# FFN gate/up products from float16 halves with scales found on the chip, all split tiles kept in DRAM

## The chip, the cores and the metric

The kernel runs on one core of one Trainium2 chip. The metric is the device time of one execution in microseconds (us), as the median of several runs.

## The reference

One inference step of an encoder layer with width 1024, for 2048 new frames and 64 frames of a running stream (2112 tokens together):

```python
h = rmsnorm(x, norm1_w)
proj = h @ w_in                       # q, k, v, z, a, b of four delta-rule heads, and pool inputs
...                                   # convolution, gated delta rule in chunks, causal pooling
x = x + concatenate([o_delta, o_pool]) @ w_out
h = rmsnorm(x, norm2_w)
x = x + (silu(h @ w_gate) * (h @ w_up)) @ w_down      # 1024 -> 2816 -> 1024
y = rmsnorm(x, normf_w)
```

All inputs and outputs are float32, and the result has to be close to that of float32 arithmetic.

## The kernel before

**Split products.** TensorE is fed with operands of reduced float32 (`F32R`). To keep float32 accuracy, each operand is split into a high half, which is the value rounded to that type, and a low half, which is the rest. Each product is made of three matmuls: high by high, high by low, low by high (the loop over `(0, 0), (0, 1), (1, 0)` in `add`, line 1650). A split takes two instructions: ACT copies the value into the high half, and DVE subtracts (`wsplit`, line 567).

**Two phases.** The first phase (four token blocks of 512, the first with the 64 extra tokens) does the input projection, the heads, the pooling and the output projection, and leaves x in DRAM. The second phase is the FFN. It goes over the tokens in three blocks of 704, each as two halves of 352 columns (`N2`). Each block goes over the 2816 hidden columns as 22 tiles of 128 (`NF`), in groups of 4, 4, 4, 4, 2, 4. `gate_up(b, f)` (line 1643) makes tile f of gate and up for block b; `down` or `down_strassen` adds a finished group into the result.

**Strassen in gate and up.** For one tile, the two token halves, the two weight matrices and the two halves of the 1024 inputs make a 2x2 block product, which is done with 7 block products instead of 8 (Strassen's scheme in Winograd's form). The seven left factors are the weight tiles `FW = ("11", "S1", "S2", "12", "S3", "S4", "22")`, where 11 and 12 come from `wg`, 22 from `wu` and the S tiles are sums; the right factors are the token tiles `FH`. Each product is 4 steps over the inputs by 3 matmuls: 12 matmuls of 128x128 by 352 columns, and 84 for a tile. The products are added up in three PSUM banks (px, py, pz); ACT and DVE combine them (g1, g2, u2), ACT makes the sigmoid from exponentials and a logarithm, and DVE multiplies (`finish`, line 1664).

**Where the weight tiles come from.** `prep_strassen` (line 621) makes the seven split tiles for hidden tile f. In the first block it loads four raw tiles of 128x512 (256 KB each), POOL makes the four sums, and ACT and DVE split all seven. The four split S tiles (512 KB each) are then stored into DRAM (`gsd`). In the second and third block the S tiles are loaded back, and the other three are loaded raw and split again. Raw tiles sit in `wraw` (4 buffers) and `wraw2` (3 buffers), split tiles in `wsp` and `wsp2` (4 buffers each, one tile of 4 KB a partition for each product). `weights` keeps up to three plan entries ahead (`AHEAD = 3`, `weights_ahead`, line 735).

**The token tiles** are made by `stats2` (line 1430): x scaled by the norm weight `n2w` and the root mean square, combined by POOL, and written to DRAM (`hpd`). `load_h` (line 1519) loads and splits them: ACT the high half, DVE or POOL the low one.

**The order of the work.** No engine runs in the order of the program text. Every instruction is noted (`Machine.note`, line 107) with a rank, its position in the text, and an estimate of its length (`cost`, line 147). At the end `issue` (line 190) plays the program through in its own model: each engine takes the ready instruction with the lowest rank (some, such as evictions of PSUM, are pulled ahead by `hurry`), and the order found is emitted for each engine. On the chip each engine then follows its list in that order and waits where something is late. For TensorE `pick` (line 288) treats reduced float32 matmuls (kind "r") as the bulk, which goes in order of rank, and holds other kinds back for a while to keep them together. All DMAs are issued by the SP queue, also in one list. Buffers of a pool made with `behind=True` (`f2`, used in the FFN) come free only when the last instruction on the first phase's own buffers is done.

Of the kernel before, what the change touches and what calls it, by code (L numbers as in the profile page):

```python
# [18 lines left out]
P = 128  # L19
D = 1024  # L20
# [44 lines left out]
class Machine:  # L65
# [81 lines left out]
    def cost(self, op, name, out, ins):  # L147
# [4 lines left out]
        if op.eng == "tensor":  # L152
            dt = ins[0].dtype
            if name == "transpose":
                op.kind, op.ldw, op.occ = "f", 0.11, 0.109
            elif dt == F32:
                op.kind, op.ldw, op.occ = "f", 0.11, 0.012 + 1.651e-3 * n
            elif dt == F32R:
                op.kind, op.ldw, op.occ = "r", 0.11, 0.008 + 0.4335e-3 * n
            else:  # L160
                op.kind, op.ldw, op.occ = "h", 0.055, 0.003 + n / 2.4e3
            op.lat = op.occ + 0.2
            return
# [13 lines left out]
        elif op.eng == "scalar":  # L177
            op.lat = (0.16 if ps else 0.2) + 0.84e-3 * n + 0.095 * max(0, len(ins) - 1)
            op.occ = op.lat - 0.1
            if "accum_out" in op.call[2]:  # L180
                op.lat, op.occ = 0.6, 0.3
# [106 lines left out]
    def pick(self, ready, t, wait):  # L288

        others = sorted(x for x in ready if x[2].kind != "r")  # L290
        if others:
            first = others[0]
            held = self.last == "r" and len(others) < len(ready) and t < min(x[2].ready + self.hold(x) for x in others)
            if self.last == "r" and not held and len(others) < len(ready):
                until = min(x[2].ready + (SOON if x[0] < 0 else HOLD[1]) for x in others)
                held = any(t < x[0] <= until and x[2].kind != "r" for x in wait)
            if held:
                first = min(x for x in ready if x[2].kind == "r")
# [9 lines left out]
    def run(self, op, t):  # L308
        op.start = t
        if op.eng == "tensor":  # L310

            free, kind = self.free["tensor"], op.kind
            if self.last == kind and op.ready <= free:
                op.start = max(t, self.at + op.ldw)
            elif kind == "r":
                if op.ready <= free:
                    op.start = max(op.ready, free - (0.028 if self.last == "h" else 0.081))
                op.occ, op.lat = op.occ + 0.087, op.lat + 0.087
            elif self.last == "h":
# [50 lines left out]
def hybrid_kernel(ctx, tc, a, o):  # L370
# [88 lines left out]
    gsd = {nm: dpool.tile([NF, P, 1024], F32, tag=f"g{nm}", name=f"g{nm}") for nm in KEEP}  # L459
# [35 lines left out]
    n1w, n2w, nfw = (nw[:, i * KT : (i + 1) * KT] for i in range(3))  # L495

# [63 lines left out]
    def wtiles(nm, second=False):  # L560
# [3 lines left out]
        return (lambda: pool.tile([P, 512], F32, tag="wraw" + x, name=f"wr{nm}_{at}", bufs=3 if second else 4),  # L564
                lambda: pool.tile([P, 2, 512], F32R, tag="wsp" + x, name=f"ws{nm}_{at}", bufs=4))
# [5 lines left out]
    def prep():  # L571
# [43 lines left out]
        while due and due[0][0] != key:  # L615
            k, done = due.pop(0)
            for dst, t in done:
                nc.sync.dma_start(out=dst, in_=flat(t))
            stored.add(k)

    def prep_strassen(key):

        q = {f"{i}{j}": a[nm][key[1]][:, (j - 1) * 512 : j * 512]
             for i, nm in ((1, "wg"), (2, "wu")) for j in (1, 2)}
        raw, t, old = {}, {}, key in stored or key[1] in PRE_GU

        def get(nm, src):
            raw[nm] = wtiles(nm)[0]()
            nc.sync.dma_start(out=raw[nm], in_=q[src])

        if old:
            for i, nm in enumerate(FW):
                t[nm] = wtiles(nm, i % 2 == 1)[1]()
                if nm in gsd and key[1] in PRE_GU:
                    for j in range(2):
                        nc.sync.dma_start(out=t[nm][:, :, 256 * j : 256 * j + 256].bitcast(F32),
                                          in_=gpd[key[1], j][PRE_NM.index(nm)].rearrange("p (q n) -> p q n", q=2))
# [14 lines left out]
        gt(out=raw["S4"], in0=raw["12"], in1=raw["S2"], op=ALU.subtract)  # L652
        for i, nm in enumerate(FW):
# [267 lines left out]
    nc.sync.dma_start(out=consts, in_=a["consts"])  # L921
    names = {}
# [36 lines left out]
    idbf = cp1.tile([P, P], BF16, tag="idbf", name="idbf")  # L959
    nc.vector.tensor_copy(idbf, ident)  # L960
# [18 lines left out]
    class Front:  # L979
# [43 lines left out]
        def all(self):  # L1023
# [32 lines left out]
            mm(gb[:, : 2 * C], idbf, bc(negm2 if self.h is None else negm, 2, C), start=False, stop=True,  # L1056
# [462 lines left out]
    def load_h(b, names):  # L1519
        for nm in names:  # L1520
            for k in range(4):
# [3 lines left out]
                else:  # L1525
# [4 lines left out]
                    out=t[:, 1], in0=raw, in1=t[:, 0].bitcast(F32), op=ALU.subtract)  # L1530
# [14 lines left out]
    hA = [bp.tile([P, 6, 2, N2], F32R, tag=f"h{i}", name=f"hA{i}") for i in range(2)]  # L1545
# [17 lines left out]
    for nm in FH[3:]:  # L1563
        t = f2.tile([P, 4, 2, N2], F32R, tag=f"h{nm}", name=f"hB{nm}")
# [78 lines left out]
    def gate_up(b, f):  # L1643
# [14 lines left out]

        def sigmoid(e, x):
            act(e, x, AF.Exp, scale=-1.0)  # L1660
# [146 lines left out]

HOLD = 0.3, 3.0, 0.6
# [26 lines left out]
PRE_NM = ("S3", "S1", "S2", "S4")  # L1835
SLACK = 0.6
KEEP = ("S1", "S2", "S3", "S4")
# [118 lines left out]
```

## Time and profile before

| | us |
|---|---|
| median of 3 runs | 2296.19 (2296.04 to 2296.88) |
| span of the profiled execution | 2295.8 |
| first phase, up to the first gate/up matmul | 933.0 |
| FFN, block 0 (to the first gate/up matmul of block 1) | 449.7 |
| FFN, block 1 | 448.8 |
| FFN, block 2, to its last gate/up matmul | 422.4 |
| the rest: last down product, final norm | 41.9 |

The profiled execution's own time is its span and what lies around it; the span is 0.4 us under the median of the runs. The profile names instructions by engine (PE is the matmul array, PEld its weight loads, DVE VectorE, ACT ScalarE, POOL GpSimd, SP the queue of DMAs) and by what they write and read: `px<-hA,ws` is a matmul into px from the token tile hA and the weight tile ws (`wsS` are the S tiles, `wsd` those of the down product, `hr`, `g` and `u` the gating, `hq` its split factors, `y` the result). Nearly all instructions have the line 285, where the program emits them, so the names tell them apart. Numbers in names are left out. Reduced float32 is shown as f32 on PE. The busy time of overlapping instructions counts once.

### The profile page before, as it was taken

The page shows a single profiled execution, that of the slowest core. Times are in us where ns is not written, and L with a number is a line of the kernel's source. Part 1 is how long each engine was busy: PE and PEld are TensorE (multiplying, and loading weights), DVE is VectorE, ACT ScalarE, POOL GpSimd, SP SyncE. Part 2 cuts the span into 40 slices and gives each one's busy share as a digit, 9 for nine tenths or more (in the row PEclk, how much of TensorE's full clock was granted, in tenths as well). Part 3 has the DMA queues.
Part 4 walks back from the last instruction along what each step waited for, and adds up shares of the span by engine and source line. Part 5 has one row for each costly group of instructions (what it writes and reads, how often), then busy time and mean ns, then how long its engine had stood idle before and what let it go on. Part 6 is the DMA issues. An engine that isn't in the chain of part 4 may idle for free.

```text
span 2295.8 us, 41549 instructions
## 1 busy us (share of the span) xinstructions
PE 2271.8 (99%) x14518; PEld 2132.1 (93%) x14518; DVE 1711.3 (75%) x3129; ACT 1342.1 (58%) x3039; POOL 833.4 (36%) x893
## 2 busy tenths in 40 slices
PE   8999999999999999999999999999999999999998
PEld 8898898888787888999999999999999999999998
DVE  8989876685678896788888786866667768666576
ACT  6986866684769864565446366554334574353344
POOL 3425342453247450565434236622111453010112
PEclk9999999999999999999999999999999999999999
DMA  8755586578476767866776578778765776666653
GB/s 295 263 182 193 199 294 234 191 238 277 159 245 232 212 212 254 304 247 247 272 260 238 185 264 292 248 266 302 234 198 199 263 271 230 209 216 224 210 195 103
DMA packets 256514, 536.96 MB, mean 234 GB/s; under 512 B 30000, under 2 KB 94000, under 8 KB 256304
## 3 DMA queue, kind: packets, MB, share of 16 engines
q1 hardware_dynamic: 255728, 533.58, 69.3%
q8 instruction: 114, 1.87, 0.3%
q14 instruction: 96, 0.79, 0.1%
q10 hardware_dynamic: 576, 0.72, 0.1%
HBM read 403.62 MB, written 130.58 MB: 233 GB/s over the span
## 4 chain that ended last, share of the span: by engine, by line
PE 88%; DVE 5%; DMA 3%; ACT 2%; issue 1%; POOL 1%; SPq 0%; DVEq 0%; POOLq 0%; ACTq 0%
PE px L285 21%; PE pp L285 17%; PE pz L285 13%; PE py L285 10%; PE dx L285 8%; PE dy L285 4%; PE d L285 3%; PE dz L285 2%; PE pk_p L285 2%; PE pt_p L285 2%; PE gr_p L285 1%; DVE y L285 1%; PE py_p L285 1%; DVE h L285 1%; DMA hpd<-xt 1%
## 5 line engine op out<-in xcount | busy, mean ns | idle before, releaser
L285 PE MATMUL pp<-h,wsp 128*128 128x512 f32 (+1 forms) x2480 | 547.9, 364 | 10.0 <-DVE wsp L285 10.0
L285 PEld LDWEIGHTS pp<-h,wsp 128*128 128x128 f32 x2480 | 401.4, 189 | 58.2 <-ACT wsp L285 9.2
L285 ACT CAST ws<-wr 128x512 fp32r<-128x512 f32 x198 | 122.1, 618 | 166.7 <-PE dx L285 55.2
L285 DVE TENSOR_TENSOR ws<-wr,ws 128x512 fp32r<-128x512 f32 x198 | 173.4, 879 | 30.9 <-ACT ws L285 27.1
L285 POOL TENSOR_TENSOR q<-hr,hr 128x352 f32<-128x352 f32 x52 | 58.0, 1116 | 369.6 <-DVE hr L285 366.8
L285 ACT CAST wsd<-wrd 128x512 fp32r<-128x512 f32 (+1 forms) x120 | 62.6, 526 | 174.8 <-PE dx L285 66.8
L285 DVE TENSOR_TENSOR y<-y,dx 128x352 f32<-128x352 f32 x240 | 121.8, 517 | 57.0 <-PE dx L285 56.0
L285 PE MATMUL pz<-op,wsp 128*128 128x288 f32 (+1 forms) x768 | 163.0, 353 | 0.0
L285 PE MATMUL px<-hA,ws 128*128 128x352 f32 x792 | 145.2, 322 | 0.0
L285 ACT ACTIVATE hr<-g 128x352 f32<-128x352 f32 x132 | 65.6, 497 | 133.7 <-DVE g L285 133.5
L285 PE MATMUL py<-hA,wsS 128*128 128x352 f32 x792 | 141.5, 322 | 2.0 <-DMA wsS<-gS 1.6
L285 PE MATMUL py<-hB,wsS 128*128 128x352 f32 x792 | 141.7, 322 | 0.0
L285 PE MATMUL pz<-hB,ws 128*128 128x352 f32 x792 | 141.0, 322 | 0.0
L285 ACT CAST TV_p<-pt_p 128x512 f16<-128x512 f32 x192 | 110.4, 589 | 49.6 <-PE pt_p L285 49.2
L285 PE MATMUL px<-hA,wsS 128*128 128x352 f32 x792 | 138.5, 322 | 0.0
L285 PE MATMUL px<-hBT,wsS 128*128 128x352 f32 x792 | 137.9, 322 | 0.2 <-ACT g L285 0.2
L285 PE MATMUL px<-hBT,ws 128*128 128x352 f32 x792 | 137.7, 322 | 0.0
L285 PEld LDWEIGHTS pz<-op,wsp 128*128 128x128 f32 x768 | 120.9, 188 | 12.1
L285 PEld LDWEIGHTS py<-hA,wsS 128*128 128x128 f32 x792 | 129.4, 188 | 2.6 <-DMA wsS<-gS 1.9
L285 PEld LDWEIGHTS px<-hA,ws 128*128 128x128 f32 x792 | 130.0, 188 | 0.1
L285 PE MATMUL dy<-hq,wsdS 128*128 128x352 f32 x672 | 129.6, 322 | 0.0
L285 PEld LDWEIGHTS py<-hB,wsS 128*128 128x128 f32 x792 | 129.4, 188 | 0.0
(697 smaller groups left out, 5777.2 us busy)
## 6 DMA issues: line engine op xcount, KB each, us to landing
wsS<-gS SPq DMA_DIRECT2D x176, 512.0 KB, 4.5
wsp<-wnd SPq DMA_DIRECT2D x126, 512.0 KB, 3.8
gS<-wsS SPq DMA_DIRECT2D x88, 512.0 KB, 4.9
wsdS<-dsd SPq DMA_DIRECT2D x88, 512.0 KB, 4.4
wr<-in_wg_dram SPq DMA_DIRECT2D x132, 256.0 KB, 3.5
wnd<-wsp SPq DMA_DIRECT2D x42, 512.0 KB, 5.0
wrd<-in_wd_dram SPq DMA_DIRECT2D x68, 256.0 KB, 2.7
xd<-x2d SPq DMA_DIRECT2D x96, 176.0 KB, 4.1
```

The lines of the kernel that those rows point to most:

```text
L285: getattr(getattr(self.nc, op.eng), name)(*args, **kw)
```

## The change

- Weight and token tiles of gate and up become float16 halves. The seven weight tiles are kept in pairs, four buffers of 4 KB a partition for a hidden tile instead of seven (`new` in `prep_strassen`).
- To keep the halves in the range of float16, weights are multiplied by a power of two s for each hidden tile, and the norm weight `n2w` by another. They are found on the chip by `scale_of`: ACT squares the four raw tiles with accumulated sums, DVE copies the sums into bfloat16, PE adds them over the partitions (one matmul with a matrix of ones for each column of sums, one column wide), ACT takes logarithm and exponential to get the inverse root, and DVE masks the result down to its exponent. The split becomes an ACT copy with scale s and a DVE `scalar_tensor_tensor` (raw x s - high). The scale is taken out again in the gating: the exponential gets `neg` as its scale, and the two products of `finish` become `scalar_tensor_tensor` with `inv`.
- The first block stores all seven split tiles (three times 512 KB and once 256 KB for a hidden tile); the later blocks only load them.
- Raw tiles of odd hidden tiles get four buffers of their own (`graw`), and `wraw2` gets six buffers instead of three.
- In the planner, 16-bit matmuls of at least 288 columns are a second bulk kind "b", and the estimate for ACT instructions with accumulation depends on their size. A bfloat16 identity of the first phase falls away; its matmul uses the float16 one.

```diff
-                op.kind, op.ldw, op.occ = "h", 0.055, 0.003 + n / 2.4e3
+                op.kind, op.ldw, op.occ = "b" if n >= WIDE else "h", 0.055, 0.003 + n / 2.4e3
...
-        others = sorted(x for x in ready if x[2].kind != "r")
+        others = sorted(x for x in ready if x[2].kind not in BULK)
...
-    gsd = {nm: dpool.tile([NF, P, 1024], F32, tag=f"g{nm}", name=f"g{nm}") for nm in KEEP}
+    gsd = {i: dpool.tile([NF, P, 2048 if i < 6 else 1024], F16, tag=f"g{i}", name=f"g{i}") for i in range(0, 7, 2)}
...
+    def scale_of(out, squares, n, top, ps):
+
+        cols = cpool.tile([P, 4], BF16, tag="sqb", name=f"sqb{machine.n}", bufs=2)[:, :n]
+        nc.vector.tensor_copy(cols, squares)
+        for i in range(n):
+            mm(ps[:, :1], ones_b, cols[:, i : i + 1], start=i == 0, stop=i == n - 1)
+        act(out, ps[:, :1], AF.Ln, bias=tiny, scale=1.0 / top**2)
+        act(out, out, AF.Exp, scale=-0.5)
+        bits = out.bitcast(mybir.dt.int32)
+        nc.vector.tensor_single_scalar(bits, bits, 0x7F800000, ALU.bitwise_and)
+
+    def weigh_norm():
+
+        sq = cpool.tile([P, 4], F32, tag="sq", name="sqn", bufs=2)
+        junk = cpool.tile([P, KT], F32, tag="junkn", name="junkn")
+        act(junk, n2w, AF.Square, accum_out=sq[:, :1])
+        scale_of(nscale, sq[:, :1], 1, 2.0**13 / D**0.5, bank(0, "nscale"))
+        ts(n2w, n2w, nscale, None, ALU.mult)
...
-        return (lambda: pool.tile([P, 512], F32, tag="wraw" + x, name=f"wr{nm}_{at}", bufs=3 if second else 4),
-                lambda: pool.tile([P, 2, 512], F32R, tag="wsp" + x, name=f"ws{nm}_{at}", bufs=4))
+        return (lambda: pool.tile([P, 512], F32, tag="wraw" + x, name=f"wr{nm}_{at}", bufs=6 if second else 4),
+                lambda: pool.tile([P, 2, 2, 512] if pair else [P, 2, 512], dt, tag="wsp" + x, name=f"ws{nm}_{at}", bufs=4))
...
-        if old:
-            for i, nm in enumerate(FW):
-                t[nm] = wtiles(nm, i % 2 == 1)[1]()
...
-                elif nm in gsd:
-                    nc.sync.dma_start(out=flat(t[nm]), in_=gsd[nm][key[1]])
-                else:
-                    get(nm, nm)
-                    wsplit(t[nm], raw[nm], 512, nc.vector)
-            return t
-        for nm, src in (("11", "11"), ("S1", "21"), ("22", "22"), ("12", "12")):
-            get(nm, src)
+        def new(i):
+            pair = wtiles("".join(FW[i : i + 2]), i % 4 == 2, F16, True)[1]()
+            t.update((nm, pair[:, j]) for j, nm in enumerate(FW[i : i + 2]))
+            return pair.rearrange("p i q n -> p (i q n)")[:, : 1024 * len(FW[i : i + 2])]
+
+        if key in stored:
+            for i in range(0, 7, 2):
+                nc.sync.dma_start(out=new(i), in_=gsd[i][f])
+            return t
+        sq = cpool.tile([P, 4], F32, tag="sq", name=f"sq{f}", bufs=2)
+        junk = wq["pool"].tile([P, 512], BF16, tag="junk", name=f"junk{f}")
+        for i, (nm, src) in enumerate((("11", "11"), ("S1", "21"), ("22", "22"), ("12", "12"))):
+            raw[nm] = wq["pool"].tile([P, 512], F32, tag="graw", name=f"gr{nm}_{f}", bufs=4) if f % 2 else wtiles(nm)[0]()
+            nc.sync.dma_start(out=raw[nm], in_=q[src])
+            act(junk, raw[nm], AF.Square, accum_out=sq[:, i : i + 1])
...
+        scale_of(s, sq, 4, 2.0**13, psp.tile([P, 512], F32, tag="mm", name=f"ws{f}", bufs=PSM))
+        ts(neg, s, nscale, -1.0, ALU.mult, ALU.mult)
+        nc.vector.reciprocal(neg, neg)
+        ts(inv, neg, -1.0, None, ALU.mult)
...
         for i, nm in enumerate(FW):
-            t[nm] = wtiles(nm, i % 2 == 1)[1]()
-            wsplit(t[nm], raw[nm], 512, nc.vector)
-        due.append((key, [(gsd[nm][key[1]], t[nm]) for nm in FW if nm in gsd]))
+            if i % 2 == 0:
+                kept.append((gsd[i][f], new(i)))
+            hi, lo = t[nm][:, 0], t[nm][:, 1]
+            act(hi, raw[nm], AF.Copy, scale=s)
+            stt(lo, raw[nm], s, hi, ALU.mult, ALU.subtract)
+        due.append((key, kept))
...
-    hA = [bp.tile([P, 6, 2, N2], F32R, tag=f"h{i}", name=f"hA{i}") for i in range(2)]
+    hA = [bp.tile([P, 6, 2, N2], F16, tag=f"h{i}", name=f"hA{i}") for i in range(2)]
...
         def sigmoid(e, x):
-            act(e, x, AF.Exp, scale=-1.0)
+            act(e, x, AF.Exp, scale=neg)
...
         def finish(i, g, u):
             e = raw[:, i]
-            tt(e, e, g, ALU.mult)
-            tt(e, e, u, ALU.mult)
+            stt(e, e, inv, g, ALU.mult, ALU.mult)
+            stt(e, e, inv, u, ALU.mult, ALU.mult)
...
+BULK, WIDE = ("r", "b"), 288
```

More of the change, by code (lines that the diff above doesn't have):

```diff
@@ L312, in run @@
             free, kind = self.free["tensor"], op.kind
-            if self.last == kind and op.ready <= free:
+            narrow = ("b", "h")
+            if (self.last == kind or kind in narrow and self.last in narrow) and op.ready <= free:
                 op.start = max(t, self.at + op.ldw)
@@ L316, in run @@
                 if op.ready <= free:
-                    op.start = max(op.ready, free - (0.028 if self.last == "h" else 0.081))
+                    op.start = max(op.ready, free - (0.028 if self.last in narrow else 0.081))
                 op.occ, op.lat = op.occ + 0.087, op.lat + 0.087
-            elif self.last == "h":
+            elif self.last in narrow:
                 op.occ, op.lat = op.occ + 0.054, op.lat + 0.054
```

48 lines of the change are left out of this document (26 added, 22 removed).

## The prediction, made before the changed kernel was run

> **What bounds the kernel now.** I read the busy shares first, then four stretches of the span, then the waits of PE, and last the single starts of matmuls.
>
> ```profile
> span 2295.8 us, 41549 instructions
> PE 2271.8 (99%) x14518; PEld 2132.1 (93%) x14518; DVE 1711.3 (75%) x3129; ACT 1342.1 (58%) x3039; POOL 833.4 (36%) x893
> ```
>
> ```profile
> 933.00:1016.50 83.50, 83.10 (x516) 82.31 (x515) 72.92 (x94) 57.08 (x120) 45.59 (x35) 1.00 0.83 297
> 1016.50:1382.70 366.20, 365.79 (x2281) 365.22 (x2280) 304.04 (x493) 185.46 (x383) 160.19 (x123) 1.00 0.69 243
> 1382.70:1831.50 448.80, 446.87 (x2782) 445.39 (x2781) 314.24 (x561) 221.69 (x469) 140.15 (x137) 1.00 0.75 247
> 1831.50:2253.90 422.40, 422.05 (x2632) 421.52 (x2631) 281.36 (x504) 200.89 (x419) 92.41 (x88) 1.00 0.68 221
> ```
>
> ```profile
> PE py L285 <- DMA wsS<-gS: 1.6, 1, 1.6
> PE dz L285 <- DVE y L285: 0.9, 3, 0.3
> ```
>
> The stretches (columns: bounds and length, then busy us of PE, PEld, DVE, ACT, POOL, then clock, DMA share, GB/s) are the FFN up to the last gate/up matmul: block 0 in two parts, block 1, block 2. In all four PE lacks 3.1 us of 1320.9, at full clock, and the list of its waits from 935 to 2260 us holds these two and 0.6 us more. So here the time is the number of matmuls times the step from one start to the next. The weight loads are busy all the time as well, but they lie under the matmuls: the steps below grow with the columns, not with the loads.
>
> **The step that is removed and the one that comes.** Gate and up are 7 products of 12 matmuls for each of 22 tiles in 3 blocks: 5544 matmuls of 352 columns, in groups of 792 like the first row. The timeline rows after it are start, length, instruction and count.
>
> ```profile
> L285 PE MATMUL px<-hA,ws 128*128 128x352 f32 x792 | 145.2, 322 | 0.0
> ```
>
> ```profile
> 889.74 43.45 PE L285 MATMUL pz<-op,wsl 128*128 128x512 f32 x191
> 933.03 2.08 PE L285 MATMUL px<-hA,ws 128*128 128x352 f32 x12
> 934.95 2.08 PE L285 MATMUL py<-hA,wsS 128*128 128x352 f32 x12
> ```
>
> ```profile
> 415.04 0.63 PE L285 MATMUL pp<-h,wsp 128*128 128x512 f32 x2
> 415.51 0.28 PE L285 MATMUL pt_p<-Yt_p,TV_p 128*128 128x128 f16 x2
> ...
> 415.75 0.28 PE L285 MATMUL pt_p<-Yt_p,TV_p 128*128 128x128 f16 x2
> ...
> 416.14 0.22 PE L285 MATMUL pf_p<-TV_p,Wl_p 128*128 128x128 f16 x1
> 416.16 0.71 PE L285 MATMUL pp<-h,wsp 128*128 128x512 f32 x2
> ```
>
> ```profile
> 757.54 0.27 PE L285 MATMUL gb_p<-negm,idbf 128*128 128x256 bf16 x1
> 757.65 0.39 PE L285 MATMUL py_p<-TV_p,Wh_p 128*128 128x128 f16 x4
> ```
>
> Reduced float32 (shown as f32): twelve matmuls of 352 columns start within 934.95 - 933.03 = 1.92 us, 160.0 ns each; 512 columns take (933.03 - 889.74) / 191 = 226.7. The difference, 66.7 ns for 160 columns, is 0.417 ns a column, so 13.3 ns of the 160.0 are a fixed part. 16-bit operands: from the fifth to the twelfth matmul of the run at 415 us are 7 steps in 0.39 us, 55.7 ns for 128 columns. 128 x 0.417 is 53.3, so the fixed part is 2.4 ns; the 256 columns of 757.54 took 110 ns, fixed part 3.3. A 16-bit matmul of 352 columns is not in this trace. Its bounds: its columns alone, 146.7 ns, and the 128-column step scaled in proportion, 153.2. Between them I take 146.7 plus 2.4 to 3.3, 149.5, because both 16-bit rows fit it. That removes 10.5 ns x 5544 = **58.2 us** (37.7 to 73.7 by the bounds), a third of it in block 0.
>
> **What is added on PE.** First, changes of type. The down products and the norm sums stay reduced float32, and PE takes what is ready, so the two kinds alternate. The pair of 512-column matmuls ahead of the 16-bit run is 0.63 us long, the pair after it 0.71, and that pair starts 0.03 after the last 16-bit start rather than 0.056; on the way in, the last 512 columns take 0.24 to the next start and the first four 16-bit steps 0.24 rather than 0.22: some 0.08 us there and back. Going through the whole timeline after 933 us I count 143 places where a gate/up matmul and another one are neighbours, from the first to the last of these rows:
>
> ```profile
> 984.92 0.32 PE L285 MATMUL rpn<-hin,ones 128*128 128x352 f32 x1
> ...
> 2253.77 19.96 PE L285 MATMUL d<-h3l,wsd 128*128 128x352 f32 x122
> ```
>
> About 71 round trips x 0.08 = **5.7 us** (4 to 8, since the order will differ). Second, the scale: per tile of block 0 four matmuls of one column with a full 128x128 weight load. The nearest rows are the 16-bit steps (0.056 each) and the 12-column float32 matmuls below, 7 steps in 0.95 - 0.25, 0.10 each. The weights are 16 bit, so I take 0.06 x 4 = 0.25 per tile, 22 tiles **5.5 us** (4.9 to 8.8). The start gets one such chain for the norm weights, some 0.5 us (0 to 2), where PE waits anyway.
>
> ```profile
> 43.27 0.95 PE L285 MATMUL pc<-consts,Rt 128*128 128x12 f32 x8
> ```
>
> **What is added on DVE, ACT and POOL, and what covers it.** In blocks 1 and 2 every tile loses three ACT casts and three DVE splits and gets four slightly longer DVE operations; its loads fall from 4 x 512 + 3 x 256 KB to 3 x 512 + 256 KB. All that only falls, under a full PE; the one DMA wait of 1.6 us may go. In block 0 each tile gets four ACT squares with accumulator reads, a logarithm and an exponential, five DVE operations on one to four columns, seven splits as scalar_tensor_tensor, and four such in the gating.
>
> ```profile
> L285 DVE TENSOR_TENSOR y<-y,dx 128x352 f32<-128x352 f32 x240 | 121.8, 517 | 57.0 <-PE dx L285 56.0
> L285 DVE SCALAR_TENSOR_TENSOR y<-y,nw,rf 128x352 f32<-128x352 f32 x16 | 8.4, 577 | 1.5 <-ACT rf L285 1.5
> ```
>
> ```profile
> L285 DVE TENSOR_SCALAR kn_p<-kn_p x32: 155/169/783, 61.7 to 813.1; 128x2 f32<-128x2 f32 x32
> ```
>
> ```profile
> 809.50 0.20 ACT L285 ACTIVATION_READ_ACCUMULATOR ktl_p<-ptk_p 128x1 f32 x1
> 809.59 0.28 ACT L285 ACTIVATE ktl_p<-ptk_p 128x128 f32<-128x128 f32 x1
> ...
> 810.34 0.31 ACT L285 ACTIVATE kn_p<-kn_p,epsc 128x2 f32<-128x2 f32 x1
> 810.53 0.62 ACT L285 ACTIVATE osq_p__2643<-po_p__2533 128x512 f32<-128x512 f32 x1
> ```
>
> The three-operand form takes 577 ns against 517, +0.06 each, so DVE gets 11 x 0.06 + 5 x 0.17 = 1.5 us per tile. A square of 512 columns is 0.62 us long and its read 0.09 behind it (809.50 to 809.59), the two small functions 0.31 at most: ACT gets 4 x 0.6 + 0.6 = 3 us per tile. In the first six tiles that is 57 + 18 = 75 us of work for 78 us (below), in the rest of block 0 some 235 for 350. Cover is there, but thin at first.
>
> DVE is closer, because it does not work alongside POOL. Here POOL runs two sums from 948.57 to 951.72, and a DVE product that takes 0.52 undisturbed, started at 950.50, ends 0.4 after POOL's second:
>
> ```profile
> 948.57 3.15 POOL L285 TENSOR_TENSOR wrS<-wrS,wr 128x512 f32<-128x512 f32 x2
> ```
>
> ```profile
> 950.50 1.60 DVE L285 TENSOR_TENSOR hr<-hr,u 128x352 f32<-128x352 f32 x1
> ```
>
> The groups of 933 to 1016.5 us, the first six tiles with no down product between them, say how much of this there is:
>
> ```profile
> L285 DVE TENSOR_TENSOR wsS<-wrS,wsS 128x512 fp32r<-128x512 f32 x21 | 22.3, 1085 | 1.0 <-ACT wsS L285 1.0
> L285 DVE TENSOR_TENSOR ws<-wr,ws 128x512 fp32r<-128x512 f32 x16 | 18.1, 1129 | 1.9 <-ACT ws L285 1.9
> L285 DVE TENSOR_TENSOR hr<-hr,g 128x352 f32<-128x352 f32 x11 | 9.1, 824 | 0.0
> ```
>
> ```profile
> L285 POOL TENSOR_TENSOR wrS<-wrS,wr 128x512 f32<-128x512 f32 x10 | 14.8, 1484 | 1.1 <-DVE ws L285 0.7
> L285 POOL TENSOR_TENSOR r<-r,sq7n 128x352 f32<-128x352 f32 x2 | 2.5, 1253 | 0.1
> ```
>
> ```profile
> L285 DVE TENSOR_TENSOR ws<-wr,ws x198: 676/693/1791, 925.7 to 2240.9; 128x512 fp32r<-128x512 f32 x198
> L285 POOL TENSOR_TENSOR wrS<-wr,wrS x44: 1284/1571/1755, 923.1 to 1341.7; 128x512 f32<-128x512 f32 x44
> ```
>
> With the undisturbed lengths of the last two rows (0.52 and 0.89 for 352 columns): 37 splits x 0.69, 24 products and splits of the gating (the 11 shown, and 13 in two smaller groups) x 0.52, 20 sums of POOL (two groups of 10) x 1.29 and 14 norm sums (seven groups of 2) x 0.89 make 25.5 + 12.5 + 25.8 + 12.5 = 76 of 83.5 us for a resource that one of the two holds at a time. The Trainium skill, SBUF — State Buffer, section "SBUF: two separate sides", states just this: a DVE operation with two SBUF inputs and a GpSimd one take an exclusive lock for the whole instruction. The trace agrees (0.52 became 1.60), and by that rule the stall below is 7 us; by the busy share of DVE alone it would be nothing.
>
> After the change PE wants these six tiles in 83.5 - 6 x 84 x 0.0105 = 78 us, and the pair needs 76 + 53 x 0.06 = 79. Some of it can go elsewhere: the norm sums come later in the order, tiles with odd number have raw buffers of their own, and six instead of three buffers take the sums, so two tiles' sums (10 us) can run in this gap of POOL:
>
> ```profile
> 923.12 1.74 POOL L285 TENSOR_TENSOR wrS<-wr,wrS 128x512 f32<-128x512 f32 x1 [37.31 <-DMA wrS<-in_wu_dram]
> ```
>
> Against that stands the first tile: its split now waits for all four raw tiles and the scale. I put **7 us** of new PE idle into block 0 (0, if the buffers cover all, to 19.4 = 1848 x 0.0105, if the block keeps its old pace). The waits added are: PE's four small matmuls for the DVE copy of the sums of squares, with the running gate/up matmuls queued behind them; ACT's first split for the scale, with the evictions of px and py behind it; DVE for the exponential, with the additions that free PSUM behind it.
>
> **Sum.** -58.2 + 5.7 + 5.5 + 0.5 + 7.0 = -39.5 us on the span of 2295.8: 2256.3. The profiled execution took about as long as the median of 2296.19 (0.4 lies around the span), so I predict **2256 us**.
>
> **Rivals.** *Block 0 is bound by DVE, POOL and ACT.* For it: 76 of 83.5 us held already, and ACT at 75 of 78. Against it: from 1016.5 to 1382.7 DVE is busy 304 of 366, and the buffers deepen. Then block 0 keeps its pace: 2256 + 12 = 2268, to about 2285 where some of the 22 x 1.5 us of added DVE work shows too. *The chain of the scale is exposed* (slower). Square and read 0.8, copy 0.17, matmuls 0.25, logarithm and exponential 0.31 each, mask 0.17, and five hand-offs, 0 to 0.3 each by the waits of PE for DVE above, say 0.15: 2.8 us per tile of block 0. If PE stands in front of its small matmuls, or the first split comes too late, in all 22 tiles, that is 61 us in place of the 7: 2310. It outweighs the gain from 46.5 / 22 = 2.1 us per tile. Against it: tiles are prepared some three steps ahead, and with paired buffers eight slots hold two tiles rather than one. *The type gives nothing.* If the fixed 13.3 ns belong to the 352-column accumulation and not to the type, only the added work stays: 2296 + 5.5 + 0.5 + 7 = 2309. The two 16-bit rows speak against it. The Trainium skill, FP8 and Floating Point Precision, section "TensorE Precision Notes", speaks for it: half-precision and reduced float32 both pass the array in the same narrow internal form. By that alone the sum is 2309; the rows, 55.7 and 110 ns, do not bear it out as a rule on time. *More is gained*: the step near 147 and no idle, 2235 to 2243.
>
> **Chances.** Forecast (2243 to 2267) 0.66; block 0 bound by the other engines 0.18; exposed chain 0.05; no gain from the type 0.04; more gained 0.07. The range that leaves 2 in 10 out at most: 2243, where the 16-bit step is 149 and nothing stalls, to 2277, where block 0 gains nothing and the small matmuls and type changes are at their upper bounds (8.8 and 8). Changes within 0.2% (4.6 us) can't be told from none: faster 0.89, same 0.03, slower 0.08.
>
> **What would show it.** The seven gate/up groups must appear as f16 with starts 149 to 150 ns apart, 1.79 us per twelve; 153 or more would break the main term. Blocks 1 and 2 (448.8 and 422.4 us) should each shorten by about 19.4 - 2 us, with PE full. Block 0 (449.7) should shorten by less, 3 to 12 us, with PE waits on the scale's copy, the splits or POOL's sums of 7 us together; if PE waits there for 20 us, the other engines bind. If the first gate/up matmul starts several us after the last output projection, the scale of the first tile is exposed.

## The result, and the profile after

The changed kernel takes 2259.51 us in the median of 4 runs (2257.41 to 2261.72), the kernel before beside it 2296.53 (2296.04 to 2300.72). The ratio, estimated from all runs and so not quite the quotient of the two medians, is 0.9834, with a 95% interval of 0.982 to 0.9847: 1.7% faster, 3.5 us above the predicted 2256. The profiled run has a span of 2259.3, 36.5 us less than the 2295.8 before.

The first fence holds the head of the page after, the second the stretches of the FFN (block 0, block 1, block 2 to its last gate/up matmul; columns as in the prediction).

```profile
span 2259.3 us, 41012 instructions
```

```profile
936.55:1385.38 448.83, 437.74 (x2874) 334.39 (x2875) 386.89 (x689) 315.12 (x703) 191.27 (x157) 0.99 0.70 238
1385.38:1817.02 431.64, 428.97 (x2788) 330.68 (x2787) 276.83 (x496) 193.45 (x409) 138.53 (x144) 1.00 0.64 207
1817.02:2217.42 400.40, 400.40 (x2623) 303.09 (x2622) 240.93 (x436) 168.56 (x350) 78.07 (x79) 1.00 0.56 175
```

Against 449.7, 448.8 and 422.4 before, the blocks changed by -0.9, -17.2 and -22.0; the rest takes 41.9 as before. The first gate/up matmul starts 3.5 us later (936.55 against 933.03). So blocks 1 and 2 gave all of the gain, and block 0, with a third of the matmuls, almost none: PE lacks 448.83 - 437.74 = 11.1 us there, where it lacked 0.8 before.

PE's timeline of the changed kernel in block 1 (start, length, instruction, count):

```profile
1455.27 1.95 PE L285 MATMUL px<-hA,wsS 128*128 128x352 f16 x12
1457.06 1.95 PE L285 MATMUL pz<-hB,wsS 128*128 128x352 f16 x12
...
1462.43 1.95 PE L285 MATMUL px<-hBT,ws 128*128 128x352 f16 x12
1464.10 1.24 PE L285 MATMUL dx<-hq,wsd 128*128 128x352 f32 x6
1465.18 1.13 PE L285 MATMUL dy<-hq,wsdS 128*128 128x352 f32 x6
1466.15 1.12 PE L285 MATMUL dz<-hq,wsd 128*128 128x352 f32 x6
```

Twelve float16 matmuls take 1457.06 - 1455.27 = 1.79 us, 149.2 ns each. In the same stretch six reduced float32 ones of the same size take 1466.15 - 1465.18 = 0.97, about 161 ns each: the difference is the type's. The change of type costs next to nothing here: from 1462.43 to 1465.18 are 2.75 us, and twelve steps of 149.2 and six of 161 are 2.76.

The way into block 0, from the timelines of PE, ACT, DVE and POOL of the changed kernel (a last bracket is the idle time before and what ended it):

```profile
919.75 15.12 PE L285 MATMUL pz<-op,wsl 128*128 128x512 f32 x66
934.72 0.51 PE L285 MATMUL ws<-sqb,onesb 128*128 128x1 bf16 x8
936.55 0.47 PE L285 MATMUL px<-hA,ws11S 128*128 128x352 f16 x2 [1.33 <-ACT ws11S L285]
...
938.43 0.45 PE L285 MATMUL pz<-hB,wsS 128*128 128x352 f16 x1 [0.80 <-ACT wsS L285]
938.68 2.99 PE L285 MATMUL px<-hA,ws11S 128*128 128x352 f16 x10
```

```profile
935.00 0.26 ACT L285 ACTIVATE wscale<-ws,tiny 128x1 f32<-128x1 f32 x1 [1.81 <-PE ws L285]
```

```profile
930.21 0.39 DVE L285 CAST sqb<-sq 128x4 bf16<-128x4 f32 x1 [2.39 <-ACT junk L285]
933.23 1.10 DVE L285 CAST sqb<-sq 128x4 bf16<-128x4 f32 x1 [2.63 <-ACT junk L285]
```

```profile
933.02 1.29 POOL L285 TENSOR_TENSOR grS<-grS,gr 128x512 f32<-128x512 f32 x1
```

Tile 0's sums of squares are in bfloat16 at 930.60. Its four small matmuls stand in PE's list beside those of tile 1, whose cast is done at 934.33, behind the output projection, and start at 934.72; ACT finds the scale from 935.00 and splits, and PE starts 1.83 us late. The other 1.7 us of the 3.5 lie before: the last output projection starts at 891.2 for 889.5 before, and in the profiles below, whose first phase does the same work, anywhere from 889.7 to 893.6.

The waits of PE in block 0 (total, times, longest), and the longest of them as PE and ACT see it:

```profile
PE dx L285 <- ACT wsd L285: 2.7, 1, 2.7
PE px L285 <- ACT g L285: 2.5, 3, 1.9
PE px L285 <- ACT ws11S L285: 2.2, 3, 1.3
PE rpn L285 <- ACT hin L285: 1.3, 1, 1.3
```

```profile
1157.08 1.65 PE L285 MATMUL px<-hA,ws11S 128*128 128x352 f16 x10
...
1161.86 0.24 PE L285 MATMUL ws<-sqb,onesb 128*128 128x1 bf16 x4
1164.79 0.59 PE L285 MATMUL dx<-hq,wsd 128*128 128x352 f32 x2 [2.69 <-ACT wsd L285]
...
1166.31 0.43 PE L285 MATMUL dz<-hq,wsd 128*128 128x352 f32 x1 [0.42 <-DVE g L285]
1166.58 3.64 PE L285 MATMUL px<-hA,wsS 128*128 128x352 f16 x12
```

```profile
1161.11 0.85 ACT L285 CAST hq<-hr 128x352 fp32r<-128x352 f32 x2
...
1162.91 0.26 ACT L285 ACTIVATE wscale<-ws,tiny 128x1 f32<-128x1 f32 x1
...
1164.12 0.61 ACT L285 CAST wsd<-wrd 128x512 fp32r<-128x512 f32 x1
...
1165.27 0.43 ACT L285 COPY g<-px 128x352 f32<-128x352 f32 x1
```

PE has finished px by 1158.73, but ACT works through sigmoids, casts for the down product (hq, wsd), the scale and a split first and copies px out at 1165.27; the wait of 2.69 us ends with the cast of wsd. Of what the change added, only the scale (1162.91 to 1163.40) stands between. PE has little else to do from 1162.1 to 1166.6, and then twelve matmuls take 3.45 us (the next starts at 1170.03) instead of 1.79, at a granted clock that has fallen to half:

```profile
1166.60:1169.60 3.00, 3.00 (x12) 1.60 (x12) 3.00 (x6) 2.52 (x5) 0.45 (x1) 0.51 0.44 146
```

### The profile page after: what moved, and what is told of

The parts are those of the page before. It is cut to its first block, busy times and chain, and to the rows that moved or that the text cites. A ratio compares the mean times of both kernels' runs of the same rounds, so it can differ in the third digit from the quotient of the medians.

```text
span 2259.3 us, 41012 instructions
## 1 busy us (share of the span) xinstructions
PE 2222.5 (98%) x14607; PEld 1786.3 (79%) x14607; DVE 1639.1 (73%) x3111; ACT 1358.8 (60%) x3131; POOL 803.9 (36%) x893
## 3 DMA queue, kind: packets, MB, share of 16 engines
q8 instruction: 114, 1.87, 0.3%
## 4 chain that ended last, share of the span: by engine, by line
PE 86%; DVE 6%; ACT 3%; DMA 2%; issue 1%; POOL 1%; SPq 0%; DVEq 0%; POOLq 0%; ACTq 0%
PE px L285 18%; PE pp L285 17%; PE pz L285 13%; PE dx L285 9%; PE py L285 9%; PE dy L285 5%; PE d L285 3%; PE dz L285 2%; PE pk_p L285 2%; PE pt_p L285 2%; PE gr_p L285 1%; PE py_p L285 1%; DVE y L285 1%; DVE wsS3S L285 0%; DVE hq L285 0%
## 5 line engine op out<-in xcount | busy, mean ns | idle before, releaser
L285 PEld LDWEIGHTS <-wsS 128*128 128x128 f16 x1584 | 154.2, 98 | 86.4 <-issue 4.5
L285 PEld LDWEIGHTS <-ws11S 128*128 128x128 f16 x1584 | 151.0, 98 | 88.3 <-ACT ws11S L285 3.8
L285 PEld LDWEIGHTS <-wsS3S 128*128 128x128 f16 x1584 | 154.2, 98 | 81.3
L285 PE MATMUL px<-hA,ws11S 128*128 128x352 f16 x792 | 138.5, 315 | 3.1 <-ACT ws11S L285 2.2
L285 PE MATMUL dx<-hq,wsd 128*128 128x352 f32 x560 | 137.1, 332 | 2.7 <-ACT wsd L285 2.7
L285 PE MATMUL px<-hA,wsS 128*128 128x352 f16 x792 | 131.6, 315 | 2.5 <-ACT g L285 2.5
L285 PE MATMUL py<-hA,ws11S 128*128 128x352 f16 x792 | 133.7, 313 | 0.3 <-DVE hr L285 0.2
L285 PE MATMUL dx<-hq,wsdS 128*128 128x352 f32 x672 | 132.1, 326 | 1.0 <-DVE hq L285 1.0
L285 PE MATMUL pz<-hB,wsS 128*128 128x352 f16 x792 | 131.5, 313 | 0.9 <-ACT wsS L285 0.8
L285 PE MATMUL py<-hB,wsS3S 128*128 128x352 f16 x792 | 132.2, 313 | 0.0
```

Of the source, the lines that this page charges most:

```text
L285: getattr(getattr(self.nc, op.eng), name)(*args, **kw)
```

## The experiments

Theory: the type gives the gain in every block, and in block 0 finding the scales eats it, as a wait (the chain of small steps is late) or as work (the engines have more to do). Rivals: block 0 is held by DVE and POOL whether or not scales are found; the planner's or the buffers' edits do the work. Each ratio is to the kernel before on the same chip; block 0 is counted from its first gate/up matmul to that of block 1.

**A constant scale.**

```diff
+            nc.vector.memset(s, 2.0**9)      # once, all 22 tiles; neg and inv from it
-            act(junk, raw[nm], AF.Square, accum_out=sq[:, i : i + 1])
-        scale_of(s, sq, 4, 2.0**13, ...)
```

> This kernel leaves out the finding of the weight scales: no squares, no sums of squares, no one-column matmuls, no logarithm, exponential or mask for the 22 hidden tiles; all tiles use the constant 512. The splits, the gating and the stores stay. If the finding is what keeps block 0 from getting shorter (the PE idle of 11.1 us and the start 3.5 us late), the first gate/up matmul starts at about 933, block 0 takes 434 to 437 us in place of 448.8, blocks 1 and 2 stay at 431.6 and 400.4, and the time is about 2244. If the pair DVE and POOL binds block 0 whether or not scales are found (the rival 'block 0 bound by DVE, POOL and ACT'), only the start and the small matmuls come back: about 2254.

Measured: 2245.42 us, ratio 0.9774 (0.9761 to 0.9788). Block 0 takes 435.65, PE lacks 5.7 us of it, and the first gate/up matmul follows the output projection at once. Finding the scales costs about 0.006 of 2296.5, 14 us: 13.2 in block 0 by the profiles. So the rival that DVE and POOL hold block 0 anyway is out for the 13 us; in the 5.7 that stay, the waits of PE name DVE for 4.1 and ACT for 1.5.

**The scales found, but not used.**

```diff
-        s = ...                              # of this tile
+        s = wscale[0][:, 0, f : f + 1]       # 512; the found one is left in a tile of its own
```

> Here the whole finding is still done for every tile, but nothing waits for it: splits and gating use the constant 512, as in the kernel without the finding. It separates the work of the finding from the wait for it. If the wait for the scale (its latency) is the cost, the time is that of the kernel without the finding plus the 88 one-column matmuls, some 2246. If the load on ACT and DVE is the cost, it stays near the 2259.5 of the changed kernel. My estimate is in between, 2250: the 3.5 us at the start and the first waits are latency, the waits for ACT from 940 to 1021 are load.

Measured: 2257.58, ratio 0.9822 (0.9808 to 0.9835). PE starts at once after the output projection, but block 0 takes 446.56. So most of the cost is not the wait of splits and gating for the scale but the instructions. (These still wait for one another in the engines' lists, the small matmuls for the casts and the logarithm for the matmuls; that part is not taken out here.) The difference of 1.2 thousandths to the changed kernel lies within the intervals; only the 1.83 us at the start can be seen as the wait's.

**Squares alone.**

```diff
             act(junk, raw[nm], AF.Square, accum_out=sq[:, i : i + 1])
-        scale_of(s, sq, 4, 2.0**13, ...)
```

> The constant scale again, and the sums over the partitions, the one-column matmuls, the logarithm, the exponential, the mask and the three short products are left out; only the four squares per hidden tile are done, and nothing reads their sums. It cuts the 13 us that the finding costs in block 0 into the squares (3 us of ACT per tile) and the short chain behind them. If the squares are the cost, block 0 takes 445 to 449 us and the ratio is 0.982. If the short instructions are, block 0 takes 435 to 438 and the ratio is 0.977 to 0.979; that is what the squares over a quarter of the columns, which brought nothing, let me expect.

Measured: 2247.78, ratio 0.9785 (0.977 to 0.98), block 0 438.07.

**Squares over a quarter of the columns.**

```diff
-            act(junk, raw[nm], AF.Square, accum_out=sq[:, i : i + 1])
+            act(junk[:, :128], raw[nm][:, :128], AF.Square, accum_out=sq[:, i : i + 1])
```

> The squares run over the first 128 of each raw tile's 512 columns (the target is halved, so the scale has the same size). ACT loses some 0.4 us per square, 1.6 us per hidden tile, 34 us in block 0; DVE, POOL and PE get the same instructions. If ACT's load is what costs block 0 its gain, about half of the 13 us that the finding costs there come back: block 0 at 442 to 444, the time at a ratio to the kernel before of about 0.980. If the short DVE instructions between the splits cost it (or the wait itself), block 0 stays at 446 to 449 and the ratio at 0.982 to 0.984.

Measured: 2263.22, ratio 0.985 (0.9833 to 0.9866), block 0 452.43: no gain, and above both ranges that I had given. The stretch of block 0 in these four kernels, in their order:

```profile
934.41:1370.06 435.65, 429.99 (x2795) 331.41 (x2794) 380.98 (x583) 255.09 (x499) 207.60 (x163) 1.00 0.72 249
```

```profile
936.84:1383.40 446.56, 436.10 (x2883) 335.53 (x2883) 384.82 (x693) 314.33 (x710) 203.26 (x164) 0.99 0.71 243
```

```profile
934.21:1372.28 438.07, 431.30 (x2796) 331.81 (x2795) 379.55 (x583) 305.33 (x665) 207.21 (x162) 1.00 0.72 248
```

```profile
937.14:1389.57 452.43, 438.57 (x2875) 334.25 (x2875) 378.33 (x689) 289.98 (x704) 198.26 (x157) 0.99 0.69 236
```

The squares add 305.33 - 255.09 = 50 us to ACT and 2.4 us to the block (the ratios of the two kernels, 0.9774 and 0.9785, lie within each other's intervals). The short chain behind them (casts, small matmuls, logarithm, exponential, mask, three products) adds only 314.33 - 305.33 = 9 us to ACT and 5 to DVE, and 8.5 to the block. Of these the small matmuls themselves are 2.2 (below), 3.7 are more idle time of PE (446.56 - 436.10 = 10.5 against 438.07 - 431.30 = 6.8), and in the block PE runs twice instead of once at half clock for some 3.4 us. The longest wait of the second kernel, its PE row, and ACT's rows up to it:

```profile
990.46 3.25 PE L285 MATMUL px<-hA,wsS 128*128 128x352 f16 x12 [3.79 <-ACT g L285]
```

```profile
989.17 0.50 ACT L285 ACTIVATE sq6n<-xd 128x352 f32<-128x352 f32 x1 [0.55 <-DVE hr L285]
989.96 0.45 ACT L285 COPY g<-px 128x352 f32<-128x352 f32 x1 [0.29 <-POOL r L285]
```

The copy that frees PE stands in ACT's list behind a square of the norm statistics; ACT is idle before both, by the profile until DVE and POOL are done. Such a wait does not need the short chain: the kernel with the squares alone has one of 2.93 us, for ACT's copy g too and with half clock behind it, at 978.53. That the planner's estimates, by which the squares would have been done, put the copy there is my reading and was not tested. What is shown is that the short chain costs the block more than the squares, though it is a fifth of their work on ACT; with a quarter of the squares nothing was gained. Which of the short steps costs most, and whether by the order or by the work, isn't settled.

**Three ways to place the finding better:** raw buffers of their own for the even tiles instead of the odd ones; a truer estimate of a square; both, with the chain ahead of other work.

```diff
-... if f % 2 else wtiles(nm)[0]()
+... if f % 2 == 0 else wtiles(nm)[0]()                     # even
-                op.lat, op.occ = max(0.6, op.lat + 0.1), max(0.3, op.occ)
+                op.lat, op.occ = max(0.6, op.lat + 0.1), max(0.3, op.occ + 0.23)   # square's cost
+        machine.boost = BOOST                              # ahead
         scale_of(s, sq, 4, 2.0**13, ...)
```

> The four raw buffers of their own go to the even hidden tiles instead of the odd ones, so that tile 0, the first that PE needs, loads at about 890 us, when tile 1 loads in the changed kernel, and its scale can be found under the output projection. All else is computed as before. If the late start (936.5 against 933.0) and the waits of the first tiles are the exposed scale of tile 0, the first gate/up matmul comes at 933 to 933.5 and the waits from 936 to 941 fall away: 2252 to 2255. If the load of ACT in the first six tiles sets the pace, the same idle time comes some tiles later and the time stays at 2258 to 2260.

> Only the planner's estimate of an ACT square with accumulation is changed, by 0.23 us to the 0.76 that the trace shows from one square to the next; no instruction is added or removed, only the order can differ. If the 6.2 us of PE idle from 1021.8 to 1385.4 come from an order that counts on ACT being free 0.9 us earlier per tile, the time falls by 3 to 6 us, to 2254 to 2257. If they come from the load itself, it stays within 2 us of 2259.5.

> The finding of all 22 scales stays, in a better place: raw buffers of their own for the even tiles (tile 0 first), the short chain ahead of other work, and squares planned at their measured pace. If late short instructions cost block 0 its gain, the start comes 1.8 us earlier and half of the 11 us of waits goes: ratio 0.978 to 0.980. If it is the number of instructions on ACT and DVE, only the start and some 3 us come back, as with the even tiles alone: 0.981 to 0.983.

Measured: 0.9821 (0.9808 to 0.9835), 0.9826 (0.9813 to 0.984) and 0.982 (0.9806 to 0.9835), all within the interval of the changed kernel or touching it. With even tiles the start is where it should be:

```profile
937.34 1.97 PE L285 MATMUL py<-hA,ws11S 128*128 128x352 f16 x12
```

That is 0.23 us after the last output projection matmul (937.11), and 1.83 of the start is back. The last kernel has that too, but PE still lacks 446.84 - 434.57 = 12.3 us of block 0: the idle time only moves. I had given the planner's estimate 3 to 6 us; it is worth none that can be told.

**The raw buffers taken back**, first those of the odd tiles alone, then those of the sums too.

```diff
-            raw[nm] = wq["pool"].tile(..., tag="graw", bufs=4) if f % 2 else wtiles(nm)[0]()
+            raw[nm] = wtiles(nm)[0]()
-... bufs=6 if second else 4          # second kernel only
+... bufs=3 if second else 4
```

> Only the raw buffers of the odd hidden tiles are taken away; the sums keep their six. With both taken away the kernel took 2331 us, and PE waited for the first split of the next tile some 3 us at a time. If the own raw buffers are what lets the loads, the squares and the scale of the next tile run ahead, the time is 2320 to 2331 again. If it was the three buffers of the sums, it is within 5 us of 2259.5.

> The raw buffers go back to what the kernel before has: none of their own for odd hidden tiles, three instead of six for the sums. The finding of the scale stays. If the pair DVE and POOL has only thin cover in the first six tiles (76 of 83.5 us before), tiles can no longer be summed ahead, and block 0 gets longer by 8 to 20 us: about 2270. If ACT is what binds, the buffers matter little: within 4 us of 2259.5.

Measured: 2330.19, ratio 1.0143 (1.0126 to 1.016), and 2331.08, ratio 1.0148 (1.0133 to 1.0163): both slower than before the change. It is all the odd tiles' buffers; without them the sums' three bring nothing that can be seen (taking away the three alone was not run). Block 0, its waits and one tile on ACT and PE, in the first of the two:

```profile
934.99:1452.74 517.75, 467.42 (x2878) 342.37 (x2878) 372.38 (x696) 323.68 (x714) 190.08 (x161) 0.93 0.60 209
```

```profile
PE px L285 <- ACT ws11S L285: 39.3, 16, 3.8
```

```profile
973.17 0.71 ACT L285 ACTIVATE ws<-wr,wscale 128x512 f16<-128x512 f32 x1
976.28 0.63 ACT L285 ACTIVATE junk<-wr 128x512 bf16<-128x512 f32 x1
...
988.10 0.72 ACT L285 ACTIVATE ws11S<-wr,wscale 128x512 f16<-128x512 f32 x1
```

```profile
988.87 0.77 PE L285 MATMUL px<-hA,ws11S 128*128 128x352 f16 x2 [3.59 <-ACT ws11S L285]
...
1008.58 0.77 PE L285 MATMUL px<-hA,ws11S 128*128 128x352 f16 x2 [3.76 <-ACT ws11S L285]
```

A raw buffer comes free with its split, so the loads of the next tile are issued only at 971.53, 972.16, 973.53 and 975.47, beside and behind the last splits (ACT's last copy is that of 973.17). Then come the squares (from 976.28 to 982.49), the sums, the scale and the first split (988.10). A tile takes 1008.58 - 988.87 = 19.7 us where its 84 matmuls need 12.5. Of the 69 us that block 0 gets longer, 30 are no wait: PE is busy 467 us in place of 437, at a clock of 0.93.

**Gate/up matmuls no longer planned as bulk.**

```diff
-BULK, WIDE = ("r", "b"), 288
+BULK, WIDE = ("r", "b"), 10000
```

> The planner no longer counts the gate/up matmuls as bulk; no instruction changes, only the order. Gate/up matmuls then go before down matmuls whenever they are ready, and the small ones are no longer held back. If a change of operand type costs the 0.08 us there and back that I predicted, the time moves with their number (199 neighbours of different kind now). If it costs 0.015 us, as the steps in blocks 1 and 2 suggest, the number is without effect, and only waits of PE can move the time: 2255 to 2268.

Measured: 2374.71, ratio 1.0339 (1.0324 to 1.0355), although the kinds alternate less often (172 neighbours against 198). Block 1, and the first of PE's waits in blocks 1 and 2 together:

```profile
1395.60:1877.66 482.06, 442.75 (x2787) 337.30 (x2787) 268.66 (x496) 190.01 (x404) 129.03 (x138) 0.96 0.58 183
```

```profile
PE dx L285 <- DVE g L285: 29.3, 2, 14.7
```

Block 1 gets 50 us longer, and block 2, with 456.44, 56. PE takes the gate/up matmuls of a tile first and then stands in its list before down products whose factors aren't made; the longest such wait, from 1461.97 to 1476.64, has no matmul in between. My expectation, 2255 to 2268, was far off. This experiment and the one on the raw buffers show that the gain is lost without these edits, not that they make it: before the change PE lacked 3.1 us of the 1320.9 up to the last gate/up matmul, so order and buffers alone had no more to give there.

**Only the S tiles stored.**

```diff
-                nc.sync.dma_start(out=new(i), in_=gsd[i][f])     # all four
+                act(t[nm][:, 0], raw[nm], AF.Copy, scale=...)    # 11, 12, 22: loaded raw and
+                stt(t[nm][:, 1], raw[nm], ...)                   # split again; S tiles loaded
```

> Only the S tiles are stored, as in the kernel before; blocks 1 and 2 load 11, 12 and 22 raw and split them again with the scale that block 0 found (three more ACT copies and DVE splits per tile; the loads stay as large). PE is full in these blocks, so this should cost nothing there: blocks 1 and 2 within 2 us of 431.6 and 400.4, and a ratio of 0.982 to 0.985. Had the stored tiles a part in the gain, these blocks would get longer by several us each, up to the 1.6 us DMA wait of before and the 2.7 us of waits for DVE at the end of block 1 or more.

Measured: 2259.53, ratio 0.9838 (0.9823 to 0.9853). Blocks 1 and 2:

```profile
1384.56:1813.20 428.64, 426.92 (x2782) 328.38 (x2781) 327.69 (x563) 230.77 (x470) 140.79 (x137) 1.00 0.63 205
1813.20:2215.58 402.38, 401.88 (x2630) 304.34 (x2630) 287.60 (x501) 207.94 (x417) 89.50 (x87) 1.00 0.55 175
```

DVE does 51 and 47 us more, ACT 37 and 39, and the two blocks together take 831.0 against 832.0 us. Storing all tiles saves work and no time.

**One scale for all tiles, found from tile 0**, which has raw buffers of its own.

```diff
+            if f == 0:
                 act(junk, raw[nm], AF.Square, accum_out=sq[:, i : i + 1])
...
-        s, neg, inv = (wscale[0][:, i, f : f + 1] for i in range(3))
+        s, neg, inv = (wscale[0][:, i, :1] for i in range(3))
```

> One scale is found, from hidden tile 0, and used for all 22; tile 0 has raw buffers of its own, and its chain of small instructions goes ahead of the rest. The finding for tiles 1 to 21 is left out. It should be as fast as the kernel with a constant scale: ratio 0.977, first gate/up matmul at most 0.5 us after the last output projection, block 0 at 433 to 437. If the first tiles wait for other reasons than the scale, 4 to 6 us of PE idle stay there.

Measured: 2246.61, ratio 0.9779 (0.9765 to 0.9794). PE starts at 934.42, 0.23 us after the output projection, and from there block 0 takes:

```profile
934.42:1370.56 436.14, 430.03 (x2796) 331.30 (x2795) 385.08 (x582) 255.60 (x499) 205.97 (x162) 1.00 0.72 247
```

This beats both kernels, the changed one by half a per cent, with intervals apart. It asks more of the weights: all hidden tiles must be near enough in size for one scale to keep them in the range of float16.

## Why the prediction was right, and which steps were wrong

- **The step.** 149.5 ns predicted, 149.2 measured, with the 161 ns of reduced float32 beside it. 5544 x (160.0 - 149.2) = 59.9 us for the predicted 58.2. The two 16-bit rows of the first phase were the right ones to build on. The Trainium skill, TensorE: Matmul & The Clock Gate, section "Wait — 56ns, not 53.3ns?", gives columns over 2.4 GHz plus about 2.5 ns, 149.2 for 352 columns by an estimate from it: the trace agrees.
- **The rival that the type gives nothing** is out: the same 352 columns take 161 ns in the one type and 149.2 in the other, in one kernel.
- **Blocks 1 and 2.** Predicted 17.4 us shorter each, 34.8; measured 17.2 + 22.0 = 39.2. The step alone gives 2 x 1848 x 0.0108 = 39.9. Block 1 has the smaller part because PE waits 2.7 us near its end (1.9 us in block 1 of the kernel before) and then runs at a granted clock of 0.50 from 1798.2 to 1801.5. That the lighter work and the stores bring nothing under a full PE was right, and is shown by the kernel that stores S tiles only.
- **Changes of type: 5.7 us predicted, about 1 measured.** I took 0.08 us there and back from runs of short 16-bit matmuls among 512-column ones. With 352 columns on both sides the way in costs nothing (2.75 against 2.76 us above). The way back:

```profile
1524.72 1.96 PE L285 MATMUL px<-hA,wsS 128*128 128x352 f16 x12
1526.52 1.65 PE L285 MATMUL py<-hB,wsS3S 128*128 128x352 f16 x10
```

  From 1524.72 to 1526.52 are 1.80 us for twelve steps that take 1.79 elsewhere: 0.01 each time.
- **Small matmuls: 5.5 us predicted, 2.2 measured.** 0.06 each was too much; four of them between gate/up matmuls move the next one by 0.10 us, so 22 x 0.10:

```profile
1065.48 0.24 PE L285 MATMUL ws<-sqb,onesb 128*128 128x1 bf16 x4
1065.58 1.50 PE L285 MATMUL px<-hBT,ws 128*128 128x352 f16 x9
```

- **PE idle in block 0: 7 us predicted, 11.1 - 0.8 = 10.3 measured, and it was priced too low in kind.** Two things hang on each wait that I left out. A matmul's recorded end lies 0.31 us after its start, so the step at a wait is longer than the idle shown; over the 20 steps of block 0 that take more than 0.3 us that is 3.4 us (0.65 before, over 4). And after the two bunches of waits at 936 and 1162 us some twenty matmuls ran at half rate: (2.83 - 1.49) + (3.45 - 1.79) = 3.0 us, with 2.83 for the ten from 938.68. With the 1.83 us at the start, the stalls cost 10.3 + 2.75 + 3.0 + 1.83 = 17.9 us, not 7.
- **Block 0 shorter by 3 to 12 us** was wrong: 0.9. By the steps: 1848 x 0.0108 = 20.0 gained; 10.3 + 2.75 + 3.0 lost to waits and what follows them, 2.2 to small matmuls; 0.9 us of the rest I can't place.
- **Who binds block 0.** I had put DVE and POOL first. The four longest groups of PE's waits, 8.7 us, all name ACT, and with the constant scale 5.7 us of idle stay. "Cover is there, but thin at first" (ACT, 75 of 78 us) was the better reading. Its sum is loose: a square and its read are 0.62 + 0.09 by the rows beside it, so 3.5 us a tile and not 3; measured are (314.33 - 255.09) / 22 = 2.7. Yet it isn't the sum of the work either: 50 us of squares on ACT cost 2.4.
- **The exposed chain** sits where I said it would, before the first split, and is enough to make the kernel slower than before. That its price, 2.8 us a tile, is near the (517.75 - 448.83) / 22 = 3.1 without the odd raw buffers is luck. Of the 3.1 only 1.8 are longer waits (PE lacks 50.3 us of that block for 11.1); most of the rest is PE at half clock, which had no term. And the chain there, from the last square's read at 982.49 to the first split at 988.10, takes 5.6 us, because its short steps stand in line behind the gating on ACT and DVE and behind twelve matmuls on PE. What failed is the cover I named. "Tiles are prepared some three steps ahead, and with paired buffers eight slots hold two tiles" counts the slots of split tiles; the raw buffers decide. Those I had counted only as cover for POOL's sums.
- **What had no price at all** is the planner's second bulk kind. Left out, it costs 115 us, more than all else together. A line that changes an order has to be costed by what the order would be without it.

The forecast came out near because the misses cancel. Better than predicted by some 10 us: the step 1.7, types 4.7, small matmuls 3.3. Worse by some 13: the stalls of block 0 and its start 10.9, the first phase 1.7. That the two sums nearly meet is luck.

## What to carry to other kernels

Read the step from one start to the next for each operand type, and a change of type is a multiplication; that part can be trusted. When a quantity has to be found from data before the data can be used, count the buffers that the raw data stay in while it is being found: one set more turned 1.4% slower into 1.7% faster. And find such a quantity once if once will do: here a few short instructions per tile cost a full PE 8.5 us, more than the long squares, and one scale for all tiles saved 0.5%.

## What was not expected of the hardware

**A cast of four columns waits for POOL.** The cast at 933.23 above takes 1.10 us and ends at 934.33, when POOL's sum of 933.02 ends (934.31). By the timelines of the two engines all 22 casts fall into two kinds: 11 start while POOL is at work and end 24 to 28 ns after its instruction (the one at 930.21, with 0.39 us, among them); the other 11 take 0.15 to 0.17 us. In block 0 these casts mean 0.47 us, where I had counted 0.17, and the other short instructions of the chain keep their length, with POOL at work or not:

```profile
L285 DVE CAST sqb<-sq 128x4 bf16<-128x4 f32 x20 | 9.4, 468 | 0.8 <-ACT junk L285 0.7
...
L285 DVE RECIPROCAL wscale<-wscale 128x1 f32<-128x1 f32 x21 | 3.4, 162 | 0.6
```

I had applied the lock of DVE and POOL only to operations with two inputs. The Trainium skill, SBUF — State Buffer, section "Who interferes with whom", also names copies and casts among those that can take the shared pair: the trace agrees. It names `tensor_scalar` too, under conditions on the operands; the mask, of one column, took 133 to 155 ns throughout. Whether the cast would escape the wait on ACT wasn't tried.

**Short waits halve the clock.** Waits of 2.69 and 0.42 us with 1.1 us of work between them were followed by 3 us at a granted clock of 0.51, and so were the waits of 1.33 and 0.80 us around 937 (ten matmuls in 2.83 us from 938.68). By the clock record of the trace these two stretches at half rate are 938.0 to 941.4 and 1166.7 to 1170.1, 3.4 us each, so each costs PE some 1.5 us beyond the waits. The Trainium skill, TensorE: Matmul & The Clock Gate, section "Part 1: The HAM clock gate (the "warmup" mystery)", puts the drop after an idle window of about 3.4 us; here no single wait was that long, so idle time that some work interrupts can bring the drop too. A wait of 1.87 us by itself, up to 1247.89, brought none (granted clock 1.00 from 1244 to 1252). How much idle time within what stretch is enough can't be told from these runs.
